# The last two attention-output jobs and the output projection's operands: from an order written by hand to one made by the scheduler

## The chip, the cores and the metric

The kernel runs on one core of one Trainium2 chip. A core has five engines with instruction queues of their own: TensorE (PE, matrix products; its weight loads are listed as PEld), VectorE (DVE), ScalarE (ACT), GpSimd (POOL) and SyncE (SP), which here only issues transfers. ACT issues some transfers as well (ACTq in the profile, SPq for SP's). Each queue is worked off strictly in order: an instruction that waits for a semaphore holds up all that stands behind it on its queue. The metric is the device time in microseconds (us) of one execution, median of the runs shown.

## The reference, cut to what matters

One decoder block over a sequence of 2048 positions and a width of 1024, all in float32. Two branches (a gated linear recurrence, and a dilated windowed attention) are each projected back to the width of the model, merged with two sigmoid gates, and sent through one more projection:

```python
y_rnn  = (hr * jax.nn.silu(z_rnn)) @ w_out_rnn[l]
y_attn = (o * jax.nn.silu(z_attn)) @ w_out_attn[l]
merged = jax.nn.sigmoid(g_r + bg_r) * y_rnn + jax.nn.sigmoid(g_a + bg_a) * y_attn
x = x + gate[:, None, :] * (merged @ w_o[l])
return rms_norm(x, g_final)
```

The change concerns the last half of `y_attn`, the merge that goes with it, and what is prepared for `merged @ w_o`.

## The kernel before, in words

**Precision.** A float32 operand is split into a rounded high part and the rest, the low part. One product is three matmuls (`mm3`, all recorded on L150): high by high, high by low, low by high. The high part is made by ACT (`hi_act`, L158), the low part by POOL (`lo_pool`, L164) or DVE (`lo_dve`, L167), as a subtraction of two operands in SBUF.

**The jobs.** `steps(jobs)` is a generator that does the two branch projections, transposed: a job is (weights, operand, column block n of 512 positions). There are four jobs for the recurrence (`yaT`) and four for the attention (`oT`). A job has 8 row blocks m of the result (tiles of 128x512, in PSUM under the name pj), and each row block has 8 k-steps of one `mm3`, so 24 matmuls. A `next()` on the generator issues one k-step and what hangs on it. Six jobs and the heads of attention are interleaved by hand; the last two jobs, (oT, 2) and (oT, 3), follow alone. Their 16 row blocks are called b0 to b15 in this document (t = 48 to 63 in the code).

For each row block the generator also issues:

- the weights, in two halves of four k each, into one of four buffers S0 to S3 (b0 uses S0 and S1, b1 S2 and S3, b2 S0 and S1 again). From b1 on they come unsplit from `wR` (L1673), two row blocks ahead, and `split_w` makes their two parts: high on ACT, low on DVE.
- the gates (`load_g`, L1712): two tiles of 128x512, named fg with four buffers, for the sigmoid gate (`gaT`) and for the already merged recurrence (`mrT`), loaded at k = 3 of the row block itself.
- the evacuation (`evict`): at k = 1 of the next row block DVE multiplies the PSUM tile by the first gate tile (L1717) and adds the second (L1719).
- the result's way to memory (`store`, L1724, into `meT`) at k = 7 of the next row block.
- loads (`load_y`, into R0 to R3) and splits (`split_y`) of the next job's operand yh, yl, spread over the steps by the tables `LOAD_Y` and `SPLIT_Y`.

**The projection's operands.** `merged @ w_o` runs as a seven-product scheme on 2x2 blocks. Its right side consists of seven operands (B11, B21, B22 and the sums T1 to T4), each as a high and a low part. They are built from `w_o` in four steps k = 0 to 3 by `build_rows(s, k)`: load two rows of 128x1024 (`load_rows`, L1846, buffers st1 to st4, the pair st1/st2 for even k, st3/st4 for odd k), multiply both by the residual gate on POOL (`gate_rows`, L1849, `v["gate"]` in st0, itself loaded on L2065), four sums on DVE (L1861), seven high parts on ACT, and seven low parts, four on DVE and three on POOL (B22, T1, T3). The sums T1 and T2 have tiles of their own (s1, s2); T3 and T4 overwrite blocks B12 and B21.

**What sets the order.** `on(n, fn, ...)` puts a function behind the n-th of the 128 k-steps of the last two jobs, and `fire(n)` calls it. The four builds start at steps 10, 34, 74 and 98. All of it stands inside `tc.manual_schedule()`, so that each engine's queue holds its instructions as the Python code issues them. Outside that block a list scheduler of the framework orders the instructions by a time model of its own and by data dependences, engine by engine.

**After the jobs.** The generator's pools (fl, pR) are closed and a new one (up) opened in their place; into it go four rows of x, the final norm's weights and the left operands A of the next column blocks. Then `output_pair(p)`, p = 0 to 7, does seven products of 12 matmuls each, named X, Z, W, V, X, Y, V by where they accumulate. The left operands of p = 0 (`load_left(0)`) are loaded into st1 and st2 as soon as these are free, since they depend only on an early job.

Of the kernel before, what the change touches and what calls it, by code (L numbers as in the profile page):

```python
# [10 lines left out]
F32 = mybir.dt.float32  # L11
# [4 lines left out]
ALU = mybir.AluOpType  # L16
# [73 lines left out]
def decoder_block(ctx, tc, x, c, positions, g_norm, w_mod, b_mod, w_in, b_gate, conv_w, conv_b,  # L90
# [75 lines left out]
    def lo_dve(o, i, h):  # L166
        return nc.vector.tensor_tensor(o, i, h.bitcast(F32), ALU.subtract).ins  # L167
# [1483 lines left out]
            at(e + 2, TAIL, self.store)  # L1651

    stored = set()
    RAW = 2 * KT * (NB + 2) + 1


    def steps(jobs):

        tiles = [(j, m) for j in range(len(jobs)) for m in range(KT)]
        Y, G = {}, {}  # L1660

        def load_w(x):

            if x < 2 * len(tiles):
                assert x == n_w[0]
                j, m = tiles[x // 2]
                if x <= RAW:
                    load_wd(jobs[j][0], m, x % 2)
                    return

                n_w[0] += 1
                W[x] = t = T(pS, [P, 2, KH, P], F32R, f"S{x % 4}")
                nc.sync.dma_start(t[:, 1].bitcast(F32), wR[m, x % 2])  # L1673

        def split_w(x):
            if RAW < x < 2 * len(tiles):
                raw = W[x][:, 1].bitcast(F32)
                hi_act(W[x][:, 0], raw)
                lo_dve(W[x][:, 1], raw, W[x][:, 0])

        def load_y(j, k):
            if j < len(jobs):
                w, ys, n = jobs[j]
                if ys is oT and (n, k) == (2, KT - 1):

                    Y0[False, n, k] = last_head[0].zt[:, 0].rearrange("p r j -> p (r j)")
                    return
                if ys is oT and n == 2 and k >= KH:

                    t = T(ap_, [P, KQW], F32, "kraw", bufs=4)  # L1690
                    nc.sync.dma_start(t[:, :CH], ys[k * P : (k + 1) * P, n * CH : (n + 1) * CH])
                    Y0[False, n, k] = t[:, :CH]
                    return
                assert ys is yaT or (n // 2, k, n % 2) in stored
                load_yd(ys, n, k)

        def split_y(j, k):
            if j < len(jobs):
                Y[j, k] = yh, yl = [T(fl, [P, CH], F32R, tag, bufs=NY) for tag in ("yh", "yl")]
                w, ys, n = jobs[j]  # L1700
                t = Y0.pop((ys is yaT, n, k))
                hi_act(yh[:], t[:])
                (lo_dve if k % 2 else lo_pool)(yl[:], t[:], yh[:])

        def load_g(t):
            j, m = tiles[t]
            w, ys, n = jobs[j]
            at_ = slice(m * P, (m + 1) * P), slice(n * CH, (n + 1) * CH)
            G[t] = []
            for src in (grT,) if ys is yaT else (gaT, mrT):  # L1710
                g = T(fl, [P, CH], F32, "fg", bufs=4)
                nc.sync.dma_start(g[:], src[at_])  # L1712
                G[t].append(g)

        def evict(t, ps):
            g = G[t]
            nc.vector.tensor_tensor(g[0][:], ps[:], g[0][:], ALU.mult)  # L1717
            if len(g) > 1:
                nc.vector.tensor_tensor(g[0][:], g[0][:], g[1][:], ALU.add)  # L1719

        def store(t):
            j, m = tiles[t]
            w, ys, n = jobs[j]
            nc.sync.dma_start((mrT if ys is yaT else meT)[m * P : (m + 1) * P, n * CH : (n + 1) * CH], G.pop(t)[0][:])  # L1724

        for k in range(KT):
            split_y(0, k)
        yield
        last = None
        for t, (j, m) in enumerate(tiles):  # L1730
            ps = T(pj, [P, CH], F32, "pj")
# [96 lines left out]
    def stage(i, shape, dt=F32):  # L1828
        return T(fp, shape, dt, f"st{i}")
# [3 lines left out]
    def on(n, fn, *args):  # L1833
        pend.setdefault(n, []).append((fn, args))
# [14 lines left out]
        nc.gpsimd.tensor_tensor(v[k, i][:], v[k, i][:], v["gate"][:], ALU.mult)  # L1849

    def part(name, k):
        name = {"T3": "B12", "T4": "B21"}.get(name, name)
        if name[0] == "T":
            if (name, k) not in v:
                v[name, k] = T(fp, [P, KH, P], F32, {"T1": "s1", "T2": "s2"}[name])
            return v[name, k][:].rearrange("p k j -> p (k j)")
        i, j = int(name[1]) - 1, int(name[2]) - 1
        return v[k, i][:, j * CH : (j + 1) * CH]

    def difference(name, k, a, b):  # L1860
        tt(part(name, k), part(a, k), part(b, k), ALU.subtract)  # L1861

    def high(name, k):
        hi_act(B[name][0][:, k, :], part(name, k))
# [2 lines left out]
        lo(B[name][1][:, k, :], part(name, k), B[name][0][:, k, :])  # L1867

    def build_rows(s, k):
        on(s, gate_rows, k, 0)  # L1870
        on(s + 5, gate_rows, k, 1)
        on(s + 6, high, "B11", k)
        on(s + 7, difference, "T1", k, "B12", "B11")
        on(s + 8, low, "B11", k, lo_dve)
        on(s + 11, high, "B21", k)
        on(s + 11, difference, "T2", k, "B22", "T1")
        on(s + 12, high, "B22", k)
        on(s + 12, difference, "T3", k, "B22", "B12")
        on(s + 13, high, "T1", k)
        on(s + 13, low, "B21", k, lo_dve)  # L1880
        on(s + 15, difference, "T4", k, "B21", "T2")
        on(s + 14, low, "B22", k, lo_pool)
        on(s + 15, high, "T2", k)
        on(s + 16, high, "T3", k)
        on(s + 16, low, "T2", k, lo_dve)
        on(s + 17, high, "T4", k)
        on(s + 17, low, "T1", k, lo_pool)
        on(s + 18, low, "T4", k, lo_dve)
        on(s + 19, low, "T3", k, lo_pool)

    A, ops = {}, {}
    NP = 2 * NB
# [167 lines left out]
        fire_p()  # L2060

    LAST = 2 * KT * KT
    with tc.manual_schedule():
        v["gate"] = stage(0, [P, D])
        nc.sync.dma_start(v["gate"][:], gateD[0:1, :].broadcast_to([P, D]))  # L2065
        load_rows(0)
        for k in range(KH):
            build_rows((10, 34, 74, 98)[k], k)
            if k:
                on((16, 44, 75)[k - 1], load_rows, k)  # L2070
        on(LAST - 24, load_left, 0)
        early = {}
        for p in range(NP):
            for d, fn, args in left_events(p):
                x = 7 * p + d - 4
                if p or d > 2:
                    on_p(max(x, 1), fn, *args)
                else:
                    on(LAST - 12 + 4 * (d + 1), fn, *args)
            if p:  # L2080
                on_p(max(7 * p - 12, 0), load_left, p)
            if p > 1:
                on_p(7 * p - 2, load_rows_x, p)
# [12 lines left out]
        fire_p()  # L2096
        for p in range(NP):
            output_pair(p)
        assert not after
# [30 lines left out]
```

## Time and profile before

| | us |
|---|---|
| median of 3 runs | 2249.14 (2249.02 to 2251.96) |
| profiled execution, its own time | 2252.27 |
| its span, first to last instruction | 2250.5 |
| PE busy in the span | 2183.3 (97%) |
| DVE, ACT, POOL busy | 1442.4, 1282.9, 1060.3 |

The page's busy shares are averages over stages. The part that the change touches is a stretch of some 122 us near the end, from 1964.9 us of the span, where the first matmul of b0 starts, to 2087.1, where the first product of `output_pair(0)` starts. Matmuls of one kind are merged in the timeline (x2 is two matmuls), and a matmul's length in the record is longer than its pace, because matmuls overlap in the pipeline; so the pace is read from starts.

### The profile page before, as it was taken

Reading aid. Unit: us, or ns where it says so; the run is one execution under the profiler, and the core shown is the slowest. Engines: PE = TensorE matmul, PEld = TensorE weight load, DVE = VectorE, ACT = ScalarE, POOL = GpSimd, SP = SyncE. Lnnn points to the kernel's source line nnn. Section 1 sums busy time; section 2 is a strip of 40 time slices with the busy share of each in tenths; the row PEclk is TensorE's granted clock in tenths of the full one; section 3 lists DMA queues with packets and bytes.
Section 4 is the critical chain, followed back from the end, with each engine's and each line's share of the span. In section 5 each row is a group of like instructions: output and inputs, shape, how many; then the busy total and the mean of one; then the engine's idle time right before and its main releaser. Section 6 shows DMA issues by size and latency. Waiting matters only on the chain.

```text
span 2250.5 us, 34124 instructions
## 1 busy us (share of the span) xinstructions
PE 2183.3 (97%) x11326; PEld 1843.5 (82%) x11326; DVE 1442.4 (64%) x2482; ACT 1282.9 (57%) x2554; POOL 1060.3 (47%) x784
## 2 busy tenths in 40 slices
PE   8999999999999999999999999999999998988998
PEld 5998888888778988888888877888888887866786
DVE  5839887878455715445445442666667776578887
ACT  6638678767534527556456203676778877533333
POOL 2557777667556322222222102555556655334443
PEclk9999999999999999999999999999999999998999
DMA  8467887887998368888989989888988887877543
GB/s 284 117 210 262 280 301 269 295 280 261 334 282 276 111 227 277 274 299 287 299 298 304 358 285 286 272 267 255 276 263 257 250 240 227 259 248 232 180 164 113
DMA packets 412133, 577.34 MB, mean 257 GB/s; under 512 B 72406, under 2 KB 270258, under 8 KB 410932
## 3 DMA queue, kind: packets, MB, share of 16 engines
q1 hardware_dynamic: 369748, 446.75, 63.4%
q10 hardware_dynamic: 42016, 128.36, 14.9%
q8 instruction: 90, 1.47, 0.3%
q14 instruction: 87, 0.71, 0.1%
q0 software_dynamic: 192, 0.05, 0.0%
HBM read 356.92 MB, written 218.11 MB: 256 GB/s over the span
## 4 chain that ended last, share of the span: by engine, by line
PE 52%; DMA 7%; DVE 4%; issue 4%; ACT 3%; POOL 3%; SPq 1%; ACTq 0%; POOLq 0%; DVEq 0%
PE X L150 10%; PE pj L150 10%; PE V L150 9%; PE W L150 5%; PE Z L150 5%; PE Y L150 4%; PE sc L150 4%; PE o L150 3%; DMA R<-in_w_in_dram 1%; PE pg L150 1%; PE pT L1505 1%; PE pT L1518 1%; DMA vraw<-vN 1%; DMA kraw<-qT 1%; DMA kraw<-kT 1%
## 5 line engine op out<-in xcount | busy, mean ns | idle before, releaser
L150 PE MATMUL pj<-yh,S 128*128 128x512 f32 x1024 | 376.4, 413 | 21.7 <-ACT S L158 9.0
L164 POOL TENSOR_TENSOR S<-R,S 128x512 fp32r<-128x512 f32 x168 | 255.6, 1529 | 173.6 <-ACT S L158 63.8
L150 PE MATMUL V<-T,S 128*128 128x512 f32 x1344 | 326.2, 392 | 4.8 <-DVE t L454 4.6
L150 PE MATMUL X<-T,S 128*128 128x512 f32 x1344 | 324.0, 390 | 1.4 <-POOL S L164 1.0
L150 PEld LDWEIGHTS V<-T,S 128*128 128x128 f32 x1344 | 252.9, 189 | 60.0 <-DVE t L454 3.0
L150 PEld LDWEIGHTS X<-T,S 128*128 128x128 f32 x1344 | 251.5, 188 | 55.5 <-POOL S L164 1.5
L150 PEld LDWEIGHTS pj<-yh,S 128*128 128x128 f32 x1024 | 197.9, 194 | 65.7 <-ACT S L158 11.5
L150 PE MATMUL pj<-yl,S 128*128 128x512 f32 x512 | 206.9, 404 | 10.3 <-POOL yl L164 5.6
L164 POOL TENSOR_TENSOR S<-s,S 128x512 fp32r<-128x512 f32 x92 | 140.2, 1524 | 116.3 <-ACT S L158 68.3
L1421 ACT ACTIVATE pp<-pp,st 128x256 f32<-128x256 f32 (+3 forms) x256 | 133.8, 524 | 96.5 <-DVE st L1420 95.4
L150 PE MATMUL Z<-T,S 128*128 128x512 f32 x672 | 161.9, 390 | 0.0
L150 PE MATMUL Y<-T,S 128*128 128x512 f32 x672 | 161.8, 390 | 0.0
L150 PE MATMUL W<-T,S 128*128 128x512 f32 x672 | 161.7, 389 | 0.0
L150 PEld LDWEIGHTS W<-T,S 128*128 128x128 f32 x672 | 126.0, 188 | 27.0 <-issue 0.9
L150 PEld LDWEIGHTS Y<-T,S 128*128 128x128 f32 x672 | 125.9, 188 | 26.0
L150 PEld LDWEIGHTS Z<-T,S 128*128 128x128 f32 x672 | 125.8, 188 | 26.1
L167 DVE TENSOR_TENSOR ptl<-pT,pth 128x384 fp32r<-128x384 f32 (+1 forms) x160 | 97.9, 629 | 75.8 <-ACT pth L158 73.6
L164 POOL TENSOR_TENSOR s<-R,s 128x512 fp32r<-128x512 f32 x32 | 45.4, 1418 | 201.6 <-ACT s L158 178.5
L912 DVE SCALAR_TENSOR_TENSOR xc<-xr,par,xc 128x512 f32<-128x512 f32 x96 | 98.9, 1030 | 47.3 <-ACT xc L906 45.0
L158 ACT ACTIVATE S<-R 128x512 fp32r<-128x512 f32 x168 | 101.5, 622 | 47.9 <-DMA R<-in_w_in_dram 23.1
L150 PEld LDWEIGHTS pj<-yl,S 128*128 128x128 f32 x512 | 99.7, 195 | 29.4 <-POOL yl L164 7.7
L1485 ACT ACTIVATE pp<-pp,M 128x256 f32<-128x256 f32 (+3 forms) x256 | 117.9, 522 | 9.9 <-DVE M L1608 9.9
(400 smaller groups left out, 4868.8 us busy)
## 6 DMA issues: line engine op xcount, KB each, us to landing
sD<-S ACTq DMA_DIRECT2D x196, 512.0 KB, 4.1
S<-sD SPq DMA_DIRECT2D x196, 512.0 KB, 5.0
S<-wD SPq DMA_DIRECT2D x98, 512.0 KB, 5.3
R<-in_w_in_dram SPq DMA_DIRECT2D x136, 256.0 KB, 4.3
wD<-s ACTq DMA_DIRECT2D x64, 256.0 KB, 5.2
T<-in_w_mod_dram SPq DMA_DIRECT2D x8, 1024.0 KB, 11.7
vN<-ev SPq DMA_DIRECT2D x64, 128.0 KB, 2.7
zaT<-ev SPq DMA_DIRECT2D x32, 256.0 KB, 4.4
```

The costliest lines, as they stand in the source:

```text
L150: nc.tensor.matmul(o, lhsT=l, rhs=r, start=st, stop=sp, **kw)
L158: nc.scalar.activation(o, i, AF.Copy)
L164: nc.gpsimd.tensor_tensor(o, i, h.bitcast(F32), ALU.subtract)
L167: return nc.vector.tensor_tensor(o, i, h.bitcast(F32), ALU.subtract).ins
L912: nc.vector.scalar_tensor_tensor(xc, xr[:, i : i + CH], cw(i), xc, ALU.mult, ALU.add)
L1421: nc.scalar.activation(pdst, pdst, AF.Exp, bias=m_, scale=-1.0, accum_out=l_)
L1485: nc.scalar.activation(pp, pp, AF.Copy, scale=w)
L1505: nc.tensor.transpose(pt[:, c0 + j * P : c0 + (j + 1) * P], pp[i][:, k * P : (k + 1) * P], ident)
L1518: nc.tensor.transpose(pt[:, c * P : (c + 1) * P], pp[:, half * P : (half + 1) * P], ident)
```

## The change

The block `tc.manual_schedule()` now begins after the two jobs, so that they and the building of the operands are ordered by the scheduler. Beside that: the gates of b1 to b13 are loaded at k = 3 of the row block before, those of b0, b14 and b15 at k = 0 of their own; the pairs of b2, b5, b8 and b11 go into two tiles of the name s1 and s2 that the sums no longer need; the result is stored at k = 4 instead of 7; the sums T1 and T2 overwrite blocks B22 and B11 in place, with other operands and in another order; and the low part of every fourth half of the weights (the first half of b2, b4, ... b14) is made by POOL instead of DVE.

```diff
-    RAW = 2 * KT * (NB + 2) + 1
+    TAIL0 = KT * (NB + 2)
+    RAW = 2 * TAIL0 + 1
...
-                lo_dve(W[x][:, 1], raw, W[x][:, 0])
+                (lo_pool if x % 4 == 0 else lo_dve)(W[x][:, 1], raw, W[x][:, 0])
...
             for src in (grT,) if ys is yaT else (gaT, mrT):
-                g = T(fl, [P, CH], F32, "fg", bufs=4)
+                if t >= TAIL0 and (t - TAIL0) % 3 == 2 and t < TAIL0 + 13:
+                    g = T(fp, [P, CH], F32, ("s1", "s2")[len(G[t])])
+                else:
+                    g = T(fl, [P, CH], F32, "fg", bufs=4)
                 nc.sync.dma_start(g[:], src[at_])
...
+        g_loads = {(0, 0): [0], (14, 0): [14], (15, 0): [15]}
+        for x in range(13):
+            g_loads[x, 3] = [x + 1]
...
-                if k == 3:
-                    load_g(t)
-                if k == 7 and t:
-                    store(t - 1)
+                if t < TAIL0:
+                    if k == 3:
+                        load_g(t)
+                    if k == 7 and t:
+                        store(t - 1)
+                else:
+                    if k == 4:
+                        store(t - 1)
+                    for x in g_loads.pop((t - TAIL0, k), ()):
+                        load_g(TAIL0 + x)
...
     def part(name, k):
-        name = {"T3": "B12", "T4": "B21"}.get(name, name)
-        if name[0] == "T":
-            if (name, k) not in v:
-                v[name, k] = T(fp, [P, KH, P], F32, {"T1": "s1", "T2": "s2"}[name])
-            return v[name, k][:].rearrange("p k j -> p (k j)")
+        name = {"T1": "B22", "T2": "B11", "T3": "B12", "T4": "B21"}.get(name, name)
...
-    def difference(name, k, a, b):
-        tt(part(name, k), part(a, k), part(b, k), ALU.subtract)
+    def combine(name, k, a, b, op):
+        tt(part(name, k), part(a, k), part(b, k), op)
...
     def build_rows(s, k):
-        on(s, gate_rows, k, 0)
-        on(s + 5, gate_rows, k, 1)
-        on(s + 6, high, "B11", k)
-        on(s + 7, difference, "T1", k, "B12", "B11")
...
-        on(s + 19, low, "T3", k, lo_pool)
+        sub, add = ALU.subtract, ALU.add
+        for d, fn, *args in (
+            (0, gate_rows, k, 0), (4, gate_rows, k, 1), (5, high, "B11", k), (6, low, "B11", k, lo_dve),
+            (9, combine, "T3", k, "B22", "B12", sub), (9, combine, "T2", k, "B11", "T3", add),
+            (9, high, "B22", k), (9, high, "B21", k), (10, low, "B22", k, lo_pool), (10, low, "B21", k, lo_dve),
+            (11, high, "T3", k), (11, high, "T2", k), (12, combine, "T4", k, "B21", "T2", sub), (12, low, "T3", k, lo_pool),
+            (13, low, "T2", k, lo_dve), (13, high, "T4", k), (14, combine, "T1", k, "B22", "T2", sub),
+            (15, high, "T1", k), (15, low, "T4", k, lo_dve), (16, low, "T1", k, lo_pool)):
+            on(s + d, fn, *args)
...
     LAST = 2 * KT * KT
+    v["gate"] = stage(0, [P, D])
+    nc.sync.dma_start(v["gate"][:], gateD[0:1, :].broadcast_to([P, D]))
+    load_rows(0)
+    for k in range(KH):
+        build_rows((10, 34, 74, 98)[k], k)
+        if k:
+            on((16, 44, 75)[k - 1], load_rows, k)
+    on(LAST - 24, load_left, 0)
...
+    for s in range(LAST):
+        next(fill)
+        fire(s)
+    next(fill, None)
+    fire(LAST)
+    assert not pend
     with tc.manual_schedule():
-        v["gate"] = stage(0, [P, D])
...
-        for s in range(LAST):
-            next(fill)
-            fire(s)
-        next(fill, None)
-        fire(LAST)
-        assert not pend
         pools.close("fl", "pR")
```

What the scheduler makes of it can be read from the instruction order of the changed kernel. The four builds, which stood beside b1 to b14, now stand beside b1 to b7 on every queue: the eight gate multiplications of 128x1024, the twelve low parts of POOL and the first four weight halves on POOL (b2, b4, b6, b8) follow each other on POOL, and 32 sums and low parts of the builds stand on DVE among the low parts of b1 to b8 and the evacuations. ACT issues the loads of two of the first four rows. On SP the loads of the residual gate (L2062 in the changed file) and of the first rows stand behind one more gate load, behind the first weights load of b1's second half and behind three loads of the next job's operand, which stood some 25 transfers later before. On PE the 12 matmuls of the first X product stand inside b8, and two of the first Z product ahead of b14; some k-steps of b9 and b11 stand ahead of the last k-steps of b8 and b10. All other matmuls keep their order.

More of the change, by code (lines that the diff above doesn't have):

```diff
@@ L1869, in build_rows @@
     def build_rows(s, k):
-        on(s, gate_rows, k, 0)
-        on(s + 5, gate_rows, k, 1)
-        on(s + 6, high, "B11", k)
-        on(s + 7, difference, "T1", k, "B12", "B11")
[L1874 to L1888, printed above, removed]
-        on(s + 19, low, "T3", k, lo_pool)
+        sub, add = ALU.subtract, ALU.add
[7 more added lines that the diff above has]
+            on(s + d, fn, *args)
     A, ops = {}, {}
@@ L2062, in decoder_block @@
     LAST = 2 * KT * KT
-    with tc.manual_schedule():
-        v["gate"] = stage(0, [P, D])
[L2065 to L2083, printed above, removed]
-        for s in range(LAST):
-            next(fill)
-            fire(s)
-        next(fill, None)
-        fire(LAST)
-        assert not pend
+    v["gate"] = stage(0, [P, D])
[6 more added lines that the diff above has]
+    on(LAST - 24, load_left, 0)
+    early = {}
+    for p in range(NP):
+        for d, fn, args in left_events(p):
+            x = 7 * p + d - 4
+            if p or d > 2:
+                on_p(max(x, 1), fn, *args)
+            else:
+                on(LAST - 12 + 4 * (d + 1), fn, *args)
+        if p:
+            on_p(max(7 * p - 12, 0), load_left, p)
+        if p > 1:
+            on_p(7 * p - 2, load_rows_x, p)
+    for s in range(LAST):
[4 more added lines that the diff above has]
+    assert not pend
+    with tc.manual_schedule():
         pools.close("fl", "pR")
```

## The prediction

> **What bounds the kernel now.** I read the page first, then busy time in the two halves of the stretch that changes, then the PE timeline there, then the queues that PE waits for.
>
> ```profile
> PE 2183.3 (97%) x11326; PEld 1843.5 (82%) x11326; DVE 1442.4 (64%) x2482; ACT 1282.9 (57%) x2554; POOL 1060.3 (47%) x784
> ...
> 1964.90:2026.70 61.80, 50.57 (x193) 38.37 (x192) 43.40 (x50) 19.18 (x34) 22.58 (x12) 0.92 0.77 251
> 2026.70:2087.10 60.40, 52.68 (x193) 39.45 (x192) 50.52 (x55) 20.96 (x37) 26.16 (x14) 0.86 0.71 218
> ...
> 1999.81:2008.14 8.33, 8.33 (x25) 6.58 (x25) 4.37 (x7) 2.25 (x4) 0.00 (x0) 0.65 0.56 187
> ```
>
> PE is the bound, but not here. In each half (b0 to b7, b8 to b15) it does 192 matmuls in 61.8 and 60.4 us; columns after the length are PE, PEld, DVE, ACT, POOL, granted clock, DMA.
>
> ```profile
> 1964.67 0.61 PE L150 MATMUL pj<-yh,S 128*128 128x512 f32 x2
> ...
> 1982.02 0.62 PE L150 MATMUL pj<-yh,S 128*128 128x512 f32 x2
> ...
> 1993.08 0.73 PE L150 MATMUL pj<-yh,S 128*128 128x512 f32 x2 [2.64 <-DVE S L167]
> ...
> 1999.81 0.80 PE L150 MATMUL pj<-yh,S 128*128 128x512 f32 x1 [4.16 <-ACT S L158]
> ...
> 2002.96 0.63 PE L150 MATMUL pj<-yl,S 128*128 128x512 f32 x1
> ...
> 2004.24 0.63 PE L150 MATMUL pj<-yl,S 128*128 128x512 f32 x1
> ...
> 2009.05 0.39 PE L150 MATMUL pj<-yl,S 128*128 128x512 f32 x1
> ...
> 2009.73 0.39 PE L150 MATMUL pj<-yl,S 128*128 128x512 f32 x1
> ...
> 2037.68 0.79 PE L150 MATMUL pj<-yl,S 128*128 128x512 f32 x1 [1.67 <-DVE yl L167]
> ...
> 2060.07 0.62 PE L150 MATMUL pj<-yh,S 128*128 128x512 f32 x1 [2.71 <-ACT S L158]
> ...
> 2087.11 0.39 PE L150 MATMUL X<-B11h,st 128*128 128x512 f32 x1
> ...
> 2104.53 0.73 PE L150 MATMUL X<-B11h,st 128*128 128x512 f32 x2 [0.49 <-DVE st L167]
> ```
>
> At full clock a k-step of three takes 2009.73 - 2009.05 = 0.68 us, so a row block takes 5.44 and a half 43.5. After the 4.16 us wait a k-step takes 1.28, with a granted clock of 0.65 on the mean of the next 8.33 us. The halves therefore lose 61.8 - 43.5 = 18.3 and 60.4 - 43.5 = 16.9 us, 35.2 in all, to waits for split operands and to the slow clock behind them. That is the most the change can win in the jobs.
>
> The splits are late since DVE and POOL hold each other up, and since queues wait for loads:
>
> ```profile
> 1972.27 4.70 POOL L1849 TENSOR_TENSOR st<-st,st 128x1024 f32<-128x1024 f32 x2 [6.30 <-DMA st<-in_w_o_dram]
> 1987.41 1.71 POOL L164 TENSOR_TENSOR B22l<-st,B22h 128x512 fp32r<-128x512 f32 x1 [10.44 <-issue]
> 1992.44 5.58 POOL L1849 TENSOR_TENSOR st<-st,st 128x1024 f32<-128x1024 f32 x2
> 2020.03 1.28 POOL L164 TENSOR_TENSOR yl<-R,yh 128x512 fp32r<-128x512 f32 x1 [6.22 <-ACT yh L158]
> ...
> 1987.28 0.69 DVE L1861 TENSOR_TENSOR s<-st,s 128x512 f32<-128x512 f32 x1
> 1987.88 1.79 DVE L1861 TENSOR_TENSOR st<-st,st 128x512 f32<-128x512 f32 x1
> 1992.95 0.68 DVE L1717 TENSOR_TENSOR fg<-pj,fg 128x512 f32<-128x512 f32 x1
> 1995.75 2.82 DVE L1861 TENSOR_TENSOR st<-st,s 128x512 f32<-128x512 f32 x1
> ```
>
> A gate multiplication takes 2.35 us alone (4.70 for two) and 2.79 beside DVE; a low part on POOL takes 1.28 alone, 1.71 beside DVE. A DVE operation on two SBUF operands takes 0.69 alone, but 1.79 and 2.82 beside these: it ends when POOL's instruction ends, so DVE gets one such operation for each POOL instruction. An evacuation out of PSUM keeps its 0.68.
>
> ```profile
> 1961.54 0.80 SPq L1712 DMA_DIRECT2D fg<-mrT  x1
> ...
> 1963.67 0.58 SPq L2065 DMA_DIRECT2D st<-gateD  x1
> 1965.58 0.47 SPq L1673 DMA_DIRECT2D S<-wR  x1
> ...
> 1964.31 7.89 DMA st<-in_w_o_dram
> 1978.88 5.89 DMA fg<-mrT
> 1985.58 3.83 DMA fg<-mrT
> 2093.45 9.02 DMA A<-meT
> ...
> ACT S L158 <- DMA S<-wR: 22.3, 12, 4.4
> DVE fg L1719 <- DMA fg<-mrT: 3.5, 2, 2.6
> ```
>
> Transfers take 3.8 to 9 us to land, by how many are under way; the last two rows are waits in the stretch (total, times, longest).
>
> **The sum, first half.** The number of instructions hardly changes: four sums for four in each build, and seven low parts go from DVE to POOL. What changes is place. The builds' eight gate multiplications and twelve low parts, with four of the seven weight halves, now fill POOL's queue from b2 to b8, and PE needs its entries: b2, b4 and b6 cannot pass their third matmul before POOL has reached their low part.
>
> Start: SP now reaches the residual gate's load behind the weights load of 1965.58 and four further loads; it went out at 1963.67. The program's semaphores let each transfer go out only when the one eight issues before it has landed, so the load waits for the landing of the added gate load, which follows that of 1961.54 at about 1962.4. With 5.89 in flight that is 1968.3; I take 1968.5, and 7.89 for the load itself gives a first gate multiplication at 1976.4 (1974.4 with 5.89, 1977.6 with 9.02). Before it was 1972.27.
>
> POOL's order from there, with 2.7 for a multiplication (mostly beside DVE) and 1.71 for a low part: four multiplications, B22, then b2's low part: 10.8 + 3.4, done at 1990.6. PE would be there at 1964.9 + 2 x 5.44 = 1975.8, so b2 waits some 14 us; b2 passed that point at about 1982.0 before. Next T3 and B22 (3.4), 0.6 for a high part, T3 (1.7), 1.9 until DVE has done two more sums and ACT a high part, T1 (1.7), 3.4 for the next row (its load goes out beside T1 and takes 5), one multiplication (2.6), T1 and b4's low part (3.0): 18.3, at 2008.9. Then two multiplications, B22, one multiplication, T3: 2.7 + 2.7 + 1.6 + 2.6 + 1.6 = 11.2, at 2020.1. The low part of b5's first half stands on DVE behind eight operations of this build, of which five pair with these POOL entries; four more at 0.6 follow: 2022.5. PE would be in b5 at 2014, so this is the second long wait, and the last. What is left of b5 to b7, 70 matmuls at 0.227, takes 15.9, and the slow clock behind the wait costs 2.4 (in the rows at 2000, 0.60 a k-step for four). b8 starts at 2040.8, against 2026.7: 14.1 us later.
>
> **Second half.** No build is left there. DVE has some five operations of 0.69 in a row block of 5.44, POOL one low part in two. A weights half is freed 12 k-steps (8.2 us) before its successor is needed: a landing of 3.83 to 4.5, 0.63 on ACT, and 0.69 or 1.28 make 5.2 to 6.4, so these loads are covered; if SP brings one more than 2 us late, PE waits. The operand splits of the new job, on which b8 waited (1.67 is the longest of several), now have the 12 hoisted matmuls of X, 2.7 us, to stand behind, and b9's first k-steps. I leave 1 us of waits: 43.5 + 1.0 + 14 x 0.227 (X and two of Z) = 47.7. The last job ends at 2088.5 against 2087.1: +1.4.
>
> Gates a row block sooner and the store at k = 4 take the 3.5 us wait for mrT off DVE; that stands in the 16.9 already. In-place sums cost the same operations.
>
> **After the jobs.** X's 12 matmuls look like a gain of 2.7 us. But the next start of PE, 2104.53, hangs on the A loads (9.02 in flight), which SP issues only behind the last store and five loads into the new pool. These count from the end of b15: 17.4 us. With X and two of Z gone, PE has 58 x 0.227 = 13.2 us of work there in place of 16.3 + 0.5, so it waits about 3.7 us and the hoisted matmuls win nothing. The last evacuation goes out some 0.5 us sooner, since DVE is free. The slow clock behind that wait: at least 0 (2.64 at 1993.08 was followed by 0.73 for two, full speed), at most 2.4 (as at 2000); I take 1.2.
>
> [...]
>
> Sum: +1.4 - 0.5 + 1.2 = +2.1 on the profiled execution's 2252.27, 2254.4. The median lies 3.1 below that execution, so for the median 2251.2.
>
> **Rivals.** *Faster.* The build's chain is shorter: POOL runs at its lone prices and loads land as in the quiet stretch. Start 1974.4; 4 x 2.35 + 2 x 1.28 = 12.0; then 14.7 and 9.6 instead of 18.3 and 11.2; the four DVE operations 2.4: b5 goes on at 2013.1 instead of 2022.5, and the time is 2241.8. It decides from 6.5 us on. For it: the pair at 1972.27 ran alone. Against: 32 DVE operations of the builds stand beside POOL's 24.
>
> *Slower.* SP's queue: a store waits for its evacuation, a gate load for the store's landing in the same buffer, and the weights of the next row block stand behind both. ACT already waits 22.3 us in 12 times for wR loads, 1.9 each; if five of b9 to b15 wait 1.9 beyond their 2 us of slack: +9.5, at 2260. It decides at +2.5, two such waits. Against: DMA is at 0.71 there and falls when the rows are loaded earlier.
>
> *Half-true.* The hoisted X does win its 2.7 us, if the A loads land sooner than 17.4 us behind b15: 2248.
>
> *Dearer pairs.* The 18 POOL entries up to b5 cost their price and DVE's in full, 1.28 + 0.69 = 1.97 instead of 1.71: 18 x 0.24 = 4.3, at 2255.4. [...] The trace shows 1.79 and 2.82 with one shared end, less than the sum.
>
> **The numbers.** Forecast 0.36, faster 0.27, slower 0.27, half-true 0.04, dearer pairs 0.06. Forecast: 2251, own range 2246 to 2256. The range reaches to both rivals: 2241 to 2263. A measurement of this kernel tells about 0.2% (4.5 us) from no change. Below 2244.6: the faster rival, 0.27. Above 2253.6: slower, dearer pairs and a tenth of the forecast's 0.36 or so: 0.36. Between: 0.37.
>
> **What would show it.** Right: one PE wait of 8 us or more (or two that follow each other) in b2, with ACT or POOL S as releaser; a second of 5 us or more in b5 on DVE S; b8 some 10 to 17 us later than 2026.7; a second half within 50 us; a wait of 3 to 4 us at the second X, on DVE st. Wrong: b2's low part on POOL before 1986, then the faster rival; a second half over 55 us with releaser S<-wR, then the slower one; or a build that DVE does in less than one operation for each POOL entry.

## The result, and the profile after

The changed kernel takes 2259.36 us (median of 5 runs, 2257.27 to 2267.91) against 2249.34 (2249.02 to 2251.96) for the kernel before beside it: a ratio of 1.0048, 95% interval 1.0034 to 1.0063. It is 10 us slower, and 8 us above the forecast of 2251: outside the forecast's own range (2246 to 2256) and inside the wide one (2241 to 2263). In a later series it stood at 1.0052 (1.0032 to 1.0071).

The page of the changed kernel, its busy times:

```profile
PE 2180.0 (96%) x11326; PEld 1839.1 (81%) x11326; DVE 1436.8 (64%) x2475; ACT 1283.2 (57%) x2554; POOL 1072.7 (47%) x791
```

The work is the same; the time lies between the instructions. For the comparison I cut the stretch into three: from b0's first matmul to the 193rd matmul of the jobs (b8), from there to the jobs' last matmul, and from there to the first product X of the third column block ("the third X" in the expectations; X of the second block is "the second X"). From the third X to the last matmul every kernel below takes 116.73 us. First the changed kernel, then the kernel before, busy time by windows (length, PE, PEld, DVE, ACT, POOL, granted clock, DMA):

```profile
1961.53:2040.31 78.78, 52.89 (x193) 39.58 (x192) 62.63 (x61) 26.21 (x46) 47.65 (x26) 0.83 0.64 216
2040.31:2093.61 53.30, 49.86 (x206) 37.24 (x205) 29.54 (x38) 16.20 (x28) 13.97 (x10) 1.00 0.68 215
2093.61:2134.07 40.46, 35.87 (x145) 28.77 (x144) 25.61 (x37) 12.18 (x22) 16.66 (x11) 0.92 0.50 170
1961.53:2134.07 172.54, 138.62 (x542) 105.59 (x541) 117.78 (x135) 54.59 (x95) 78.28 (x45) 0.90 0.62 205
```

```profile
1964.90:2026.73 61.83, 50.60 (x193) 38.37 (x192) 43.43 (x50) 19.20 (x34) 22.58 (x12) 0.92 0.77 251
2026.73:2086.89 60.16, 52.44 (x193) 39.26 (x191) 50.27 (x55) 20.93 (x37) 25.95 (x14) 0.86 0.72 219
2086.89:2124.06 37.17, 36.19 (x159) 29.25 (x157) 27.99 (x38) 13.74 (x25) 19.14 (x12) 1.00 0.54 185
1964.90:2124.06 159.16, 139.23 (x542) 106.87 (x540) 121.69 (x141) 53.87 (x94) 67.68 (x37) 0.91 0.69 224
```

The stretch grew by 172.54 - 159.16 = 13.4 us: the first half by 17.0, the part behind the jobs by 3.3 though 14 matmuls fewer are left in it; the second half shrank by 6.9. That the spans differ by only 10.4 (2260.9 and 2250.5) comes from b0, which starts 3.4 us earlier in this execution, an offset that the matmuls ahead of 1550 us already have.

The PE timeline of the changed kernel, its long waits and what stands around them:

```profile
1983.32 0.79 PE L150 MATMUL pj<-yh,S 128*128 128x512 f32 x1 [8.09 <-ACT S L158]
1987.72 1.22 PE L150 MATMUL pj<-yh,S 128*128 128x512 f32 x2 [3.19 <-POOL S L164]
1999.24 1.22 PE L150 MATMUL pj<-yh,S 128*128 128x512 f32 x2 [3.34 <-DVE S L167]
2007.52 0.73 PE L150 MATMUL pj<-yh,S 128*128 128x512 f32 x2 [0.98 <-POOL S L164]
2015.53 0.50 PE L150 MATMUL pj<-yh,S 128*128 128x512 f32 x1 [2.70 <-ACT S L158]
2022.35 1.22 PE L150 MATMUL pj<-yh,S 128*128 128x512 f32 x2 [6.09 <-DVE S L167]
...
2041.49 0.74 PE L150 MATMUL pj<-yh,S 128*128 128x512 f32 x2 [0.57 <-POOL S L164]
2042.83 0.50 PE L150 MATMUL X<-B11h,st 128*128 128x512 f32 x1 [0.60 <-ACT st L158]
2071.51 0.74 PE L150 MATMUL pj<-yh,S 128*128 128x512 f32 x2 [0.51 <-DVE S L167]
2081.20 0.50 PE L150 MATMUL Z<-T2h,st 128*128 128x512 f32 x1 [1.64 <-ACT st L158]
...
2109.68 0.50 PE L150 MATMUL X<-B11h,st 128*128 128x512 f32 x1 [2.54 <-ACT st L158]
2112.47 1.22 PE L150 MATMUL X<-B11h,st 128*128 128x512 f32 x2 [2.06 <-DVE st L167]
```

b2 waits 11.3 us before its third matmul, b3 3.3, b5 8.8; then the second half runs at full clock with small waits; at the second X PE waits twice, and what follows is slow. POOL in the first half shows what b2 and b5 stood behind:

```profile
1974.15 10.17 POOL L1862 TENSOR_TENSOR st<-st,st 128x1024 f32<-128x1024 f32 x4 [9.84 <-DMA st<-gateD]
1984.29 1.71 POOL L164 TENSOR_TENSOR B22l<-st,B22h 128x512 fp32r<-128x512 f32 x1
1985.96 1.71 POOL L164 TENSOR_TENSOR S<-S 128x512 fp32r<-128x512 f32 x1
...
2005.76 1.71 POOL L164 TENSOR_TENSOR S<-S 128x512 fp32r<-128x512 f32 x1
...
2017.63 1.72 POOL L164 TENSOR_TENSOR T3l<-st,T3h 128x512 fp32r<-128x512 f32 x1
```

Four multiplications and one low part stand ahead of b2's low part (S, 1985.96). On ACT the high part of the same weights half stands behind high parts of the builds that wait for POOL's third multiplication:

```profile
1981.60 0.63 ACT L158 ACTIVATE B22h<-st 128x512 fp32r<-128x512 f32 x1 [2.12 <-DMA S<-wR]
1982.13 0.61 ACT L158 ACTIVATE B21h<-st 128x512 fp32r<-128x512 f32 x1
1982.65 0.61 ACT L158 ACTIVATE S<-S 128x512 fp32r<-128x512 f32 x1
```

The releaser named at 1981.60 had landed; that high part reads the tile whose multiplication ended at 1981.6. So PE waited for ACT first (8.09) and for POOL behind that (3.19), both held by one queue.

### The profile page after: what moved, and what is told of

Read it like the earlier page. It is cut to its first block, busy times and chain, and to the rows that moved or that the text cites. A ratio compares the mean times of both kernels' runs of the same rounds, so it can differ in the third digit from the quotient of the medians.

```text
span 2260.9 us, 34116 instructions
## 1 busy us (share of the span) xinstructions
PE 2180.0 (96%) x11326; PEld 1839.1 (81%) x11326; DVE 1436.8 (64%) x2475; ACT 1283.2 (57%) x2554; POOL 1072.7 (47%) x791
## 4 chain that ended last, share of the span: by engine, by line
PE 51%; DMA 9%; DVE 4%; issue 3%; POOL 2%; ACT 2%; SPq 1%; ACTq 0%; POOLq 0%; DVEq 0%
PE X L150 10%; PE V L150 9%; PE pj L150 7%; PE W L150 5%; PE Z L150 5%; PE Y L150 4%; PE sc L150 3%; PE o L150 3%; DMA R<-in_w_in_dram 1%; PE pg L150 1%; DMA kraw<-qT 1%; PE pT L1505 1%; DMA vraw<-vN 1%; PE pT L1518 1%; DMA S<-wR 1%
## 5 line engine op out<-in xcount | busy, mean ns | idle before, releaser
L158 ACT ACTIVATE S<-R 128x512 fp32r<-128x512 f32 x168 | 101.4, 621 | 45.7 <-DMA R<-in_w_in_dram 16.9
L1420 DVE CUSTOM_DVE_ANT_0 pp<-sc,msk 128x256 f32<-128x256 f32 (+3 forms) x256 | 104.6, 449 | 23.4 <-PE sc L150 21.3
```

The source lines that it names most:

```text
L158: nc.scalar.activation(o, i, AF.Copy)
L1420: nc.vector.tensor_tensor_reduce(pdst, s_ps, mask, 1.0, 3e38, ALU.add, ALU.min, m_)
```

## The experiments

My theory: the scheduler's order is the loss, because it packs the four builds beside b1 to b7 on every queue. The rivals: the other edits, above all the quarter of the low parts on POOL; late loads; the hoisted products. The table gives the three parts and their sum in the profiled execution, and the time against the kernel before in the same series. What was expected of a run before it ran is quoted ahead of its result.

| kernel | first half | second | to the third X | sum | ratio, 95% interval |
|---|---|---|---|---|---|
| before | 61.83 | 60.16 | 37.17 | 159.16 | |
| before_again | 61.47 | 59.37 | 37.50 | 158.34 | 1.0001 (0.9989 to 1.0013) |
| after | 78.78 | 53.30 | 40.46 | 172.54 | 1.0048 (1.0034 to 1.0063) |
| after_again | 78.08 | 55.35 | 38.71 | 172.14 | 1.0052 (1.0032 to 1.0071) |
| hand_order | 65.20 | 58.32 | 37.15 | 160.67 | 0.9994 (0.9981 to 1.0008) |
| order_alone | 81.12 | 51.61 | 39.94 | 172.67 | 1.0065 (1.0047 to 1.0083) |
| builds_2_3_by_hand | 70.64 | 60.21 | 36.97 | 167.82 | 1.0027 (1.0017 to 1.0037) |
| from_b4_by_hand | 61.50 | 60.23 | 38.33 | 160.06 | 1.0006 (0.9995 to 1.0017) |
| x_behind_b15 | 78.63 | 55.56 | 37.41 | 171.60 | 1.0052 (1.0035 to 1.0070) |
| b11_gates_elsewhere | 78.33 | 52.73 | 36.98 | 168.04 | 1.0060 (1.0047 to 1.0073) |
| left_loads_first | 77.34 | 54.63 | 32.42 | 164.39 | 1.0032 (1.0020 to 1.0043) |
| hand_order_low_on_dve | 64.26 | 57.94 | 37.99 | 160.19 | 1.0012 (1.0002 to 1.0022) |
| left_loads_first_before | 60.26 | 59.53 | 35.59 | 155.38 | 0.9990 (0.9977 to 1.0002) |
| left_loads_first_hand | 63.21 | 57.50 | 35.58 | 156.29 | 0.9998 (0.9985 to 1.0010) |

### How far a single trace can be trusted: both kernels again

> The changed kernel, unchanged, once more. If its stretch is set by its queues and not by what happens to be under way, the time from b0's first matmul to the third X repeats 172.5 us within 2, with waits at the same matmuls of b2, b3 and b5 and at the second X, wherever b0 itself lies (1958.6 to 1968.3 in the traces so far): 2257 to 2263. Rival, the stretch varies by as much as the whole time does, some 8 us, and then single traces prove little.

> The kernel before, unchanged, once more. From b0 to the third X 159.2 us within 2, and b0 itself anywhere between 1958 and 1969; 2249 within 1. Rival, the stretch varies by 5 us or more.

Sums of 172.14 and 158.34 us, each within 0.9 of the first trace. The changed kernel's long waits in b2, b3 and b5 repeat within 0.4 us. Single waits elsewhere do not: at the second X the first wait is 0.90 us in place of 2.54, a wait of 0.90 in front of b14 is new and a slow stretch follows it, and in the kernel before b4 waits 2.59 in place of 4.16. The whole times spread much wider (12 runs of the kernel before: 2245.97 to 2253.96, median 2251.07, a miss for "2249 within 1"). In the traces of this study b0 starts anywhere between 1958.6 and 1968.7, so the spread arises ahead of the stretch. That speaks for comparing stretches by trace and whole times by many runs.

### The order undone, and the order alone

```diff
+    with tc.manual_schedule():
         v["gate"] = stage(0, [P, D])
...
-    with tc.manual_schedule():
         pools.close("fl", "pR")
```

> The changed kernel with one thing undone: the block of the hand-written order encloses the two jobs again. Gates a row block sooner, stores at k = 4, sums in place and the quarter of the low parts on POOL stay. If the scheduler's order carries the loss (the first half took 78.8 us after, 61.8 before; waits of 8.1, 3.2 and 3.3 us in b2 and b3, 2.7 and 6.1 in b5), these waits go, and the second X waits no longer: 2244 to 2251, between a gain by the sooner gates and the time before. Rival, the other edits carry it, above all POOL's low parts of b2, b4, ... that stand behind gate multiplications of 2.35 us in the hand order too: 2254 to 2262.

hand_order: 2248.05 us, a ratio of 0.9994; the sum is 160.67, within 2.3 us of the kernel before. Gates a row block sooner, early stores, sums in place and the quarter on POOL together cost nothing that can be told from zero, and gain nothing, in this order. b2 still waits 2.98 us here, for a high part on ACT that waits for its weights' load; so not all of the 8.09 need come from the packed builds. The opposite, on the kernel before, moves only the block:

```diff
-    with tc.manual_schedule():
-        v["gate"] = stage(0, [P, D])
+    v["gate"] = stage(0, [P, D])
...
+    with tc.manual_schedule():
         pools.close("fl", "pR")
```

> The kernel before with one thing done: the block of the hand-written order begins after the two jobs. Gates, stores, sums and low parts stay as they were before; no low part of the weights is on POOL. If compressed builds are the cause, whatever engine makes the low parts, DVE takes POOL's place: its queue holds the builds' sums and low parts, each of which pairs with a POOL entry, ahead of the weights' low parts of b2 to b5, so b2 and b5 wait still: 2256 to 2268. Rival, the quarter of the low parts on POOL is what ties PE to POOL's queue, and without it the order costs little: 2246 to 2252.

order_alone: 2263.83 us, 1.0065: all of the loss, with no weights half on POOL. (Its first half in the table holds 12 hoisted matmuls of X as well, 2.7 us.) Its PE timeline in b2 and b4:

```profile
1989.45 0.80 PE L150 MATMUL pj<-yh,S 128*128 128x512 f32 x1 [8.25 <-ACT S L158]
1994.32 1.22 PE L150 MATMUL pj<-yh,S 128*128 128x512 f32 x2 [3.65 <-DVE S L167]
...
2018.42 1.22 PE L150 MATMUL pj<-yh,S 128*128 128x512 f32 x2 [7.08 <-DVE S L167]
```

b2 waits twice as before, with DVE named where POOL was. The other places differ: the second long wait stands in b4 (its 15th matmul) in place of b5, and b3 has none. The loss does not need the low parts on POOL; it needs the builds ahead of the low parts. The order is the cause, and the rival of the other edits falls.

### How many builds may be packed

The hand-written order begins inside the jobs, first in their middle (builds_2_3_by_hand):

```diff
-    for s in range(LAST):
+    for s in range(LAST // 2):
         next(fill)
         fire(s)
+    with tc.manual_schedule():
+        for s in range(LAST // 2, LAST):
+            next(fill)
+            fire(s)
```

> The changed kernel, but the hand-written order begins in the middle, with b8: the builds k = 0 and 1 stay compressed beside b1 to b4, the builds 2 and 3 go back beside b9 to b14, and X and Z stand behind b15. By the chain of POOL entries the waits of b2 and b3 (8.1, 3.2, 3.3 us) stay within 1 us, those of b5 (2.7 and 6.1) go with the slow clock behind them: first half 67 to 71 us in place of 78.8. Second half 54 to 60 us with two builds in it and no hoisted matmul, and no wait over 2 us at the second X: 2245 to 2252. Rival, b5 waits for its late loads and not for the builds: first half over 75 us, 2255 or more.

```profile
1979.83 0.80 PE L150 MATMUL pj<-yh,S 128*128 128x512 f32 x1 [7.84 <-ACT S L158]
1984.23 1.22 PE L150 MATMUL pj<-yh,S 128*128 128x512 f32 x2 [3.18 <-POOL S L164]
...
1995.75 1.22 PE L150 MATMUL pj<-yh,S 128*128 128x512 f32 x2 [3.37 <-DVE S L167]
```

The waits of b2 and b3 stay within 0.3 us, those of b5 are gone, and the first half is 70.64, as the chain of POOL entries said. The total missed: 2255.12 in place of at most 2252, since two builds beside b9 to b14 cost their full 60.21 there (60.16 before) and the other two are still packed. With `LAST // 4` (from_b4_by_hand):

> As builds_2_3_by_hand, but the hand-written order begins with b4: only the build k = 0 is ordered by the scheduler, k = 1 goes back beside b4 to b6. On POOL two gate multiplications stand ahead of the low part of b2's first half in place of four and the first low part of B22, on ACT one high part of the builds ahead of its high part in place of four. If the queue of the builds is what b2 waits for, the time from b0's start to b2's third matmul falls from 26.2 us by two multiplications of 2.35 to 2.8 and one low part of 1.7, 6.4 to 7.3; first half 62 to 66 us in place of 70.6, and 160 to 163 us from b0 to the third X in place of 167.8; 2247 to 2251. Rival, b2 waits for the loads that SP issues in this stretch (the residual gate, two rows of 128x1024 and the weights), which stay: the long waits of b2 stay within 2 us, 2253 or more.

2248.94 us, 1.0006; first half 61.50, sum 160.06: what hand_order has. But the reason in the expectation was half wrong. POOL and SP of this kernel, and behind them the row of SP in builds_2_3_by_hand:

```profile
1977.31 10.22 POOL L1862 TENSOR_TENSOR st<-st,st 128x1024 f32<-128x1024 f32 x4 [7.51 <-DMA st<-gateD]
1987.50 1.71 POOL L164 TENSOR_TENSOR S<-S 128x512 fp32r<-128x512 f32 x1
```

```profile
1969.08 0.82 SPq L2062 DMA_DIRECT2D st<-gateD  x1
```

```profile
1962.19 0.32 SPq L2062 DMA_DIRECT2D st<-gateD  x1
```

All four multiplications still stand ahead of b2's low part: the second build's two, the first on POOL in the hand-written part, were placed ahead of it, and why is not shown. b2's third matmul comes 21.0 us behind b0, against 25.6 in builds_2_3_by_hand (1984.23 - 1958.61). Of these 4.6 us the start of POOL's first multiplication gives 3.0 (9.0 behind b0 against 12.0, 1970.65), and the low part of B22 that is gone from its place ahead of b2's gives 1.7. The residual gate's load went out 0.8 us behind b0 in place of 3.6, because three loads of the next job's operand no longer stand ahead of it on SP. So the rival of the late loads was right for the start, and POOL's queue for the rest; both orders are the scheduler's. The other 4.5 us of the first half are b3's wait of 3.37 and the slow clock behind it, which are gone. Taken together: packing builds 2 and 3, with the hoisted products that go with it, costs 172.5 - 167.8 = 4.7 us net, packing build 1 with what comes ahead of it 7.8, and build 0 nothing that shows.

### The hoisted products

```diff
-    for s in range(LAST):
+    for s in range(LAST - 1):
         next(fill)
         fire(s)
+    with tc.manual_schedule():
+        for s in range(LAST - 1, LAST):
+            next(fill)
+            fire(s)
```

> The changed kernel, but the last k-step of b15 and all behind it stand in the hand-written order, so that no matmul of X or Z stands ahead of b15's end; DVE, ACT, POOL and SP keep the order of the changed kernel but for three low parts and one load. The trace of after has waits of 0.6 us in front of the hoisted X and 1.6 in front of the hoisted Z, and 2.5 and 2.1 us at the second X with a slow stretch of some 20 matmuls behind them. By the terms on record (the second X hangs on loads that count from b15's end; 14 matmuls by 0.227 and 1.2 of slow clock) it is 4.4 us faster than the changed kernel, 2255; with the waits and the slow stretch as the trace of after has them (2.2 + 3.2 + 3.6) it is 9 faster, 2250. Rival, the hoisted matmuls win their 2.7 us and the waits only move: 2259 to 2262.

x_behind_b15: 2261.66 us, 1.0052: not faster at all. The waits at the second X shrank to one of 0.69 us, as expected (37.41 to the third X, clock 1.00), but the second half takes 55.56 us with the 14 matmuls of X and Z gone from it. Its windows row, the wait that is new, and DVE ahead of it:

```profile
2044.99:2100.55 55.56, 48.27 (x193) 36.31 (x192) 29.13 (x36) 16.37 (x28) 14.23 (x10) 0.97 0.66 208
```

```profile
2088.18 0.47 PE L150 MATMUL pj<-yh,S 128*128 128x512 f32 x1 [3.58 <-ACT st L158]
```

```profile
2084.31 0.69 DVE L1908 TENSOR_TENSOR s<-st,st 128x512 f32<-128x512 f32 x1 [2.35 <-DMA meT<-s]
...
2087.35 0.68 DVE L1721 TENSOR_TENSOR fg<-pj,fg 128x512 f32<-128x512 f32 x1
```

X had covered the operand splits in b8 and b9, which now are waited for (0.77 and 0.84 us). And the left operand's sums (L1908) still stood early on DVE, where the first waits 2.35 us for b11's result to leave s1. b12's evacuation (L1721) stands behind them and ends at 2088.03, and b14 needs the PSUM tile that it empties: there are two of pj. The ACT instruction named as releaser ended only 0.06 us later. So b14 took over Z's wait. The waits only moved, as the rival said.

```diff
-                if t >= TAIL0 and (t - TAIL0) % 3 == 2 and t < TAIL0 + 13:
+                if t >= TAIL0 and (t - TAIL0) % 3 == 2 and t < TAIL0 + 10:
```

> As x_behind_b15, but the gates of b11 stay in fg, so that nobody needs the tile s1 between b8 and the sums of the left operand. In x_behind_b15 ACT held a high part of the left operand, which waited for a sum into s1, which waited for b11's result to leave s1; behind it on ACT stood the high part of b14's second weights half, and PE waited 3.6 us and ran some 10 matmuls at half clock. If that queue is the cause, the wait and the slow stretch go, 5.5 us: from b0 to the third X 166 us in place of 171.6, 2255 to 2257. Rival, b14's weights come late by their own load, or fg with four buffers makes later gates late: 2260 to 2263.

b11_gates_elsewhere: the trace agrees in part. The wait at b14 falls from 3.58 to 1.94 us, no slow stretch follows, and the sum falls by 3.6 to 168.04. The queue was right, but what stood on it was b12's evacuation on DVE, and not b14's weights on ACT, which only b14's 13th matmul needs. With s1 free, the evacuation ends at 2082.14 and b14 waits for the high part of its weights, whose load is late, as the rival said. The times do not agree: 2261.83, 1.0060. That s1 held up the queue is seen in the traces and not confirmed by the runs; it stays open.

### The loads behind the jobs

```diff
+        load_left(1)
         load_rows_x(0)
         load_rows_x(1)
...
-            if p:
+            if p > 1:
                 on_p(max(7 * p - 12, 0), load_left, p)
```

> The changed kernel with one order of loads turned round: the A loads of the second column block go out ahead of the four rows of x and of the norm's weights, 2.8 us sooner (2097.2 in place of 2100.0 in the trace of after) and with fewer transfers beside them. If the second X hangs on these loads, its waits (2.5 and 2.1 us) shrink to 2 in all or less, the 20 matmuls at half clock behind them (0.43 in place of 0.23 each, 4.1) go, and from b0 to the third X it takes 165 to 168 us in place of 172.5: 2252 to 2256. Rival, the evacuations of b14 and b15, behind which all these loads stand, or the rows of x that now come last, hold it up all the same: 2258 to 2262.

SP of this kernel (left_loads_first) from the last store on and its last window; behind them, from the changed kernel, the same loads on SP and the operation on DVE that waited for them:

```profile
2098.86 1.65 SPq L1728 DMA_DIRECT2D meT<-fg  x2
2100.61 1.18 SPq L1896 DMA_DIRECT2D A<-meT  x2
2101.84 3.63 SPq L1938 DMA_DIRECT2D xo<-in_x_dram  x4
```

```profile
2097.08:2129.50 32.42, 32.42 (x145) 26.85 (x143) 24.12 (x37) 11.89 (x22) 15.35 (x11) 1.00 0.60 212
```

```profile
2097.19 2.07 SPq L1938 DMA_DIRECT2D xo<-in_x_dram  x4
2099.31 0.67 SPq L2093 DMA_DIRECT2D gf<-in_g_final_dram  x1
2100.03 5.39 SPq L1896 DMA_DIRECT2D A<-meT  x4
...
2110.53 0.69 DVE L1908 TENSOR_TENSOR s<-A,A 128x512 f32<-128x512 f32 x1 [8.52 <-DMA A<-meT]
```

The A loads go out 3.5 us behind the jobs' last matmul in place of 6.4. PE never waits at the second X, the clock stays at 1.00, and the part takes 32.42 us, 8.0 and 6.3 less than in the two traces of the changed kernel. The time is 2255.14, 1.0032 against 1.0048 and 1.0052: a gain of some 4 us by the ratios, whose intervals overlap, so that it rests on the traces. In them the second X did hang on these loads, and the rows of x can wait.

### In search of a faster version

> As hand_order, with the low parts of every half of the weights on DVE, as before the change. In hand_order PE waits 3.6 us in three places for low parts on POOL that stand behind or beside gate multiplications (longest 1.7). If the quarter on POOL costs these waits and DVE has room for seven more operations of 0.69, up to 3.6 us go: 2244 to 2247. Rival, the low parts only wait on DVE instead, behind operations that pair with POOL's (1.7 to 2.9 us): 2247 to 2251.

(`lo_dve` for every half, in the hand order: hand_order_low_on_dve.) 2250.52, 1.0012: the rival. PE's 3.6 us of waits for POOL are gone, those for DVE S went from 4.8 to 8.0.

> The kernel before with the A loads of the second column block ahead of the rows of x and the norm's weights. Its trace has 1.6 us of pauses between the jobs and the third X (0.88 at the second X, 0.88 at the second Z, each less one matmul of 0.23, and three small ones): up to 1.6 us faster, 2247.5 to 2249. Rival, nothing waits for the loads alone there, and the rows of x come late in their turn: 2249 to 2251.

> hand_order with the A loads of the second column block ahead of the rows of x and the norm's weights: the same 1.6 us of pauses, on a kernel that stood at 0.9994 of the one before: 2246 to 2248, a ratio of 0.9985 to 0.999. Rival, as for the kernel before: 2248 to 2250.

The part behind the jobs takes 35.59 and 35.58 us in place of 37.17 and 37.15, as expected to the tenth; the time of the first is 2248.12, 0.9990 (0.9977 to 1.0002). It is the lowest ratio of all, and 1.6 us of it can be pointed at in the trace, but the interval still holds 1, so the time alone does not show it. The second missed: 2248.74, 0.9998, no faster than hand_order's 0.9994. No faster version was found that the times bear out.

## Why the prediction was right or wrong

The likeliest time was 2251, no change that a measurement could tell, and a time above 2253.6 had nearly the same chance (0.36 against 0.37). The kernel came out slower, within the wide range and outside the forecast's own. That the slower rival had 2260 is luck: what it names did not cost the time (below). The mechanisms of the first half were the right ones, sized somewhat too small; the step that failed is the waits of the second half. Of the five signs named for the forecast three came: the waits of b2 and of b5, and b8 13.6 us later. Two did not: the second half took 53.3 us and not at most 50, and the second X waited 2.54 and 2.06 us and not 3 to 4 in one. The sign of the faster rival, b2's low part before 1986, is met by the letter (1985.96) because b0 lay 3.4 us earlier; from b0 it is 24.4 us against 21.1. Counted from b0:

| step | forecast | measured | error added by the step |
|---|---|---|---|
| first gate multiplication | 11.5 | 12.6 (1974.15) | +1.1 |
| b2's third matmul | 25.7 | 26.2 (1987.72) | -0.6 |
| b4's low part done on POOL | 44.0 | 45.9 (2005.76 + 1.71) | +1.4 |
| T3 done | 55.2 | 57.8 (2017.63 + 1.72) | +0.7 |
| b5's third matmul | 57.6 | 60.8 (2022.35) | +0.6 |
| b8 | 75.9 | 78.8 | -0.3 |
| second half, to the Z of 2093.84 | 47.7 | 53.5 | +5.8 |
| to the second X's third matmul | 16.9 | 18.6 | +1.7 |
| slow clock behind it | 1.2 | 3.0 | +1.8 |

The errors add up to +12.2; with the forecast of +2.1, and less 0.7 for a pause at the second Z that the kernel before had and this one has not, 13.6, against the measured 13.4.

*First half.* Right: two long waits, in b2 with ACT and POOL S as releasers (8.09 and 3.19) and in b5 on DVE S (6.09, behind 2.70 on ACT S). That b8 came within 0.5 us of the forecast in absolute time (2040.31 for 2040.8) is luck; by b0 it is 2.9 late. The prices of POOL were right (2.59 mean of eight multiplications, 1.71 for a low part, for 2.7 and 1.71); what came out longer were POOL's idle times from b2's to b4's low part: 1.9, 1.9, 1.4 and 2.5 us, for high parts of T3 and T1 and for a row, where the chain had 0.6, 1.9 and 3.4.

*Second half.* "I leave 1 us of waits" is the step that failed. 206 matmuls at 0.227 make 46.8, so 53.5 has 6.8 us of pauses: 0.73, 0.77, 0.67 and 1.80 at the four waits shown (each gap less one matmul), 2.4 in twenty pauses of 0.07 to 0.26, and the rest in smaller ones. Two of the four large ones stand in front of the hoisted X and Z themselves: the prediction counted what these cover, which x_behind_b15 shows to be right, and not that they wait for their own operands in the middle of a job. The slower rival's mechanism, weights loads late on SP, is not what cost: no wait for a weights half is longer than 0.6 us here.

*After the jobs.* "The hoisted matmuls win nothing, since the A loads count from b15's end" was right, and left_loads_first shows it. But the last evacuation did not come 0.5 sooner: DVE had a left sum in front of it.

```profile
2093.03 1.78 DVE L1908 TENSOR_TENSOR s<-st,s 128x512 f32<-128x512 f32 x1
...
2095.33 0.68 DVE L1721 TENSOR_TENSOR fg<-pj,fg 128x512 f32<-128x512 f32 x1
2096.04 0.69 DVE L1723 TENSOR_TENSOR fg<-fg,fg 128x512 f32<-128x512 f32 x1
```

It ended 3.1 us behind b15's last matmul, where it was 2.4 before, and the A loads behind it followed. And the slow clock was put at 1.2, half of the 2.4 at 2000; it cost 3.0, 14 matmuls at 0.43 in place of 0.23.

*The other edits.* "In-place sums cost the same operations" and "sooner gates stand in the 16.9 already" were right as zeros: hand_order has all of them at 0.9994. The sooner gates, stores and sums were not taken apart; without the quarter on POOL the hand order stood at 1.0012, so the quarter does not lose there.

*The faster rival* failed at its first condition: the start was 12.6 us behind b0 and not 9.5. *Dearer pairs* (whose 0.24 should be 1.97 - 1.71 = 0.26) was refuted by the prices above: no low part on POOL took more than 1.85 us in the stretch of either kernel. All 36 DVE operations of 128x512 on SBUF operands that took over 0.75 us in the changed kernel's stretch ended 0.55 us behind the end of a POOL instruction (2018.14 to 2019.89, T3's at 2019.34), and not with it, as the prediction read. Where a low part or a gate multiplication ran on POOL as one of them ended, it was longer by 0.43 to 0.47 us (1.71 to 1.75 for 1.28, 2.80 for 2.35; once by 0.29), not by the whole 0.69.

## What to carry to other kernels

Where several engines feed PE through queues that are worked off in order (in x_behind_b15 a wait of 2.35 us for s1 held b12's evacuation behind it), what counted here was not the amount of preparation but how much of it stood ahead of the next thing PE needed: against hand_order one packed build was free, two cost some 7 us, four some 12, with the same instructions. A matmul that is hoisted into a wait brings the wait for its own operand with it (0.60 us at X, 1.64 at Z), and when it empties a later stage whose loads have a fixed start, it buys only a pause there (2.54 and 2.06 us). Before such a stage is costed, look at what SP issues first in it: here two loads moved ahead of five took a pause and a slow stretch away (32.42 us in place of 40.46 and 38.71).

## What the runs showed of the hardware

**The clock behind waits.** Like waits ended differently. The pair 1.76 and 0.90 in after_again was followed by half clock (matmuls 0.43 us apart in place of 0.23), and the pair 1.79 and 0.90 at the same matmuls in left_loads_first was not; the two waits at the second X, 2.54 and 2.06, were followed by a slow stretch of 6.1 us (2112.47 to 2118.6); and 0.74 us after the wait of 2.70 us in b5 ended, the clock halved (2016.27). What differs is where they lie. In each of the 14 traces the granted clock changes only at times that are whole multiples of 3.41 us apart: in the changed kernel at 1978.73, 1992.38, 1999.21, 2002.62, 2016.27, 2026.51, 2111.85 and 2118.67. Windows on this grid, from after, after_again and left_loads_first (the number behind the length is PE's busy time, the third from the end the granted clock):

```profile
2108.43:2111.85 3.42, 0.73 (x2) 0.30 (x2) 1.32 (x3) 0.63 (x1) 0.00 (x0) 1.00 1.07 380
2111.85:2118.67 6.82, 6.20 (x15) 4.85 (x16) 6.66 (x8) 2.85 (x5) 6.77 (x5) 0.50 0.05 16
```

```profile
2076.71:2080.12 3.41, 1.56 (x6) 0.67 (x4) 2.92 (x3) 1.26 (x2) 1.66 (x2) 1.00 0.09 36
2080.12:2086.95 6.83, 6.01 (x14) 4.76 (x15) 4.09 (x7) 1.78 (x3) 1.30 (x1) 0.50 0.48 137
```

```profile
2082.94:2086.36 3.42, 1.89 (x7) 1.28 (x8) 3.39 (x4) 1.73 (x3) 2.75 (x2) 1.00 0.00 0
2086.36:2089.80 3.44, 3.44 (x17) 2.85 (x16) 1.68 (x3) 0.00 (x0) 0.00 (x0) 1.00 0.73 216
```

In these rows the pauses within one window of 3.41 us add up to 2.96 us in after and 2.05 in after_again, with half clock behind them, and to 1.83 in left_loads_first, with full clock behind them (a matmul counted as 0.227 us, its pace, and not by its longer record). From b0 to the third X, over all 14 traces, the 55 windows at full clock that were followed by half clock held at least 2.02 us of pauses, and the others at full clock at most 2.12. Full clock came back behind 55 windows with at most 0.75 us of pauses (0.427 a matmul), and did not behind 53 with at least 0.79. So a wait that lay across two windows went without half clock, where 2.05 us of pauses within one did not: the 2.64 us at 1993.08 in the kernel before, which the prediction took for its lower bound, lay across 1992.03, two windows ahead of a change at 1998.86. b0 lies 0.1 to 3.3 us behind a time of this grid, by trace (0.17 in the kernel before, 3.28 in the changed one).

**Where the spread comes from.** All traces have 116.73 us from the third X to the last matmul, and the stretch of either kernel repeats within 0.9; the start of b0 moves by 10 us. What moves it lies ahead of what was studied here, and was not looked for.
